# Values as the stationary operand in the attentions of layers 0 and 1

## The chip, the cores and the metric

The kernel runs on one core of a Trainium2 chip. A core has five engines that run side by side: TensorE (PE in the profile, its weight loads PEld), VectorE (DVE), ScalarE (ACT), GpSimd (POOL) and SyncE (SP), which issues most transfers. TensorE multiplies: a stationary operand is loaded (LDWEIGHTS), a moving one streams past it (MATMUL), and the result goes to PSUM, eight banks of 128 partitions by 512 floats. The metric is the device time of one execution in microseconds.

## The reference, cut to what matters

A first block of two layers on 256 tokens and 256 context tokens, then a second block of two layers. Each of the first two layers mixes with attentions of 8 heads of 64. Layer 0 has a recurrence (gated delta rule) beside a latent attention (`blocked_attention`) for all 512 tokens; layer 1 has a neighbourhood attention with a bias and a grouped-query attention (again `blocked_attention`, 2 key/value heads) for the 256 tokens alone. What is computed in each:

```python
s = jnp.einsum('bqkgd,bskd->bkgqs', q_i, k).astype(jnp.float32) * scale
p = jax.nn.softmax(s, axis=-1).astype(v.dtype)
return jnp.einsum('bkgqs,bskd->bqkgd', p, v)
...
s_loc = jnp.einsum('bqhd,bqnhd->bhqn', q_i, kg).astype(jnp.float32) * scale + b_i[None]
s_ctx = jnp.einsum('bqhd,bshd->bhqs', q_i, k_ctx).astype(jnp.float32) * scale
p = jax.nn.softmax(jnp.concatenate([s_loc, s_ctx], -1), axis=-1).astype(v.dtype)
...
y_lat = jnp.concatenate([c_lat.reshape(b, s_len, -1), d_lat.reshape(b, s_len, -1)], -1) @ w_out
```

The concatenated heads go into the output projection `w_out`. The second block's attention is a third one, which the change leaves as it is.

## The kernel before, in words

Tokens are worked on in tiles of 128. Activations that feed a projection are held features by tokens, each as a rounded part ("hi") and a rest ("lo"), and a product in that form is three instructions, high by high, high by rest, rest by high (`mm3`, lines 549 to 551). `split` makes the two parts: a cast on ScalarE, a subtraction on VectorE.

`attend` does one attend: a pair of heads, one tile of 128 tokens. For each head it gets the scores (tokens by keys, 256 or 512 keys) in a PSUM bank, takes the row's maximum on VectorE (L672), the exponential on ScalarE with its sum (L674), transposes the probabilities on TensorE in blocks of 128 (L677) and copies them to SBUF, one head's on ScalarE (L682), the other's on VectorE (L680). Then it multiplies with the values (L688): the transposed probabilities, 128 keys by 128 tokens, are the stationary operand, the values, 128 keys by 64, the moving one, and the result in bank "po" is tokens by 64. VectorE takes the reciprocal of the sums (L691) and multiplies while it takes the result out of PSUM (L692). Probabilities and values are plain 32-bit floats, for which each product is two instructions in the trace. So that the output projection can use it, the result is later transposed (`out_features`, L701) and split.

`l0_mla` (layer 0) goes over four pairs of heads and, in each, over the four token tiles: 16 attends, the tiles of the context with 256 keys, the others with 512. Its scores contract over 128 rows. It is traced after the recurrence (`gdn_run`) and before the last modulation products (`mod_chunk`, L372, bank "gv"). `l1_mixer` has `na(t)` and `gqa(t)` for the two token tiles, four pairs each: 16 attends with 512 keys. Their scores contract over 64 rows, the two heads of a pair in partitions 0 to 63 and 64 to 127. The order in the program: a part of the projections, `na(0)`, the rest of the projections, `na(1)`, the transposes of the grouped keys and queries (`pairs_T`, L1318, bank "aux"), `gqa(0)`, `gqa(1)`.

The order in which each engine gets its instructions is not the program's. A planner simulates the program before the run, prefers what stands earlier in it, but takes what is ready, and hands out buffers as they come free (`tc.tile_pool` with a number of buffers per tag). Each engine then works through its own queue in that fixed order. In layer 1 the banks are "acc" 2, "aux" 1, "s" 2, "tp" 2, "po" 1; in layer 0 "g" 3, "s" 2, "tp" 1, "po" 1, "gv" 1. SBUF tiles "p" and "pt" have two buffers each. The weights of the next stage are loaded when this stage's buffers are closed.

Of the kernel before, what the change touches and what calls it, by code (L numbers as in the profile page):

```python
# [132 lines left out]
def cut(K, shape, dt=F32, tag=None, bufs=1):  # L133
    return sbt(K, shape, dt, tag, bufs, K.cur)
# [74 lines left out]
def aux(K):  # L209
    return bank(K, "aux")  # L210
# [446 lines left out]

def attend(K, pair, t, score, v, O, kinds=("s", "s", "tp", "tp")):  # L660


    nc = K.nc
    sm = cut(K, [128, 2], F32, "sm", 4)
    pts = []
    for hh in range(2):
        h = 2 * pair + hh
        ps, nmx = score(h, t, bank(K, kinds[hh]))
        n = ps.shape[-1]
        if nmx is None:  # L670
            nmx = cut(K, [128, 1], F32, "nmx", 6)
            nc.vector.tensor_reduce(nmx, ps, axis=AX.X, op=ALU.max, negate=True)  # L672
        p = cut(K, [128, 512], F32, "p", K.np)
        nc.scalar.activation(p[:, :n], ps, AF.Exp, bias=nmx, accum_out=sm[:, hh:hh + 1])  # L674
        tp = bank(K, kinds[2 + hh])
        for j in range(n // 128):
            nc.tensor.transpose(tp[:, j * 128:(j + 1) * 128], p[:, j * 128:(j + 1) * 128], K.ident)  # L677
        pt = cut(K, [128, 512], F32, "pt", K.np)
        if hh:
            nc.vector.tensor_copy(pt[:, :n], tp[:, :n])  # L680
        else:
            nc.scalar.copy(pt[:, :n], tp[:, :n])  # L682
        pts.append((pt, n // 128))
    po = bank(K, "po")
# [21 lines left out]
def bc(ap, shape, axis):  # L706
    return ap.unsqueeze(axis).to_broadcast(shape)
# [52 lines left out]
def l0_mla(K, O):  # L760

    nc = K.nc
# [48 lines left out]
    for pair in range(4):  # L811
        heads = {}
        for h in (2 * pair, 2 * pair + 1):
            if h % 4 == 0:
                wq = WQ.load(K.ins["w_q"], 0, 2, (h // 4) * 512, 512)
            late = "g" if pair >= 2 else None
            ps = bank(K, late or "acc")
            hs = slice((h % 4) * 128, (h % 4 + 1) * 128)
            for k in range(2):
                mm3(K, ps, wq[0][:, k, hs], wq[1][:, k, hs], qh[:, k, :], ql[:, k, :], k == 0, k == 1)  # L820
            u = cut(K, [128, 512], F32, "p", K.np)
            nc.vector.tensor_tensor(u, ps, K.c("qtab"), op=ALU.mult)
            q1, q2 = cut(K, [128, 512], FR, "q1", 2), cut(K, [128, 512], FR, "q2", 2)
            split(K, q1, q2, u)
            ps = bank(K, late or "acc")
            hs = slice(h * 64, (h + 1) * 64)
            mm3(K, ps[:64, :], wkh[:, 0, hs], wkl[:, 0, hs], ch, cl, True, True)
            k1, k2 = kh[h % 2], kl[h % 2]
            nc.scalar.copy(k1[:64, :], ps[:64, :])
            nc.vector.tensor_tensor(k2[:64, :], ps[:64, :], k1.bitcast(F32)[:64, :], op=ALU.subtract)  # L830
            heads[h] = (q1, q2, k1, k2)
        for t in range(4):
            n = 256 if t < 2 else 512

            def score(h, t, ps):
                q1, q2, k1, k2 = heads[h]
                tk = slice(t * 128, (t + 1) * 128)
                mm3(K, ps[:, :n], q1[:, tk], q2[:, tk], k1[:, :n], k2[:, :n], True, True)
                return ps[:, :n], None
            attend(K, pair, t, score, lambda h, j: vt[:, j, h * 64:(h + 1) * 64],  # L840
                   O[:, t, pair * 128:(pair + 1) * 128], ("s", "g", "tp", "g") if late else ("s", "s", "tp", "tp"))

# [476 lines left out]
    feat_split(K, hi[:, :n, tk], lo[:, :n, tk], ps[:, :n * 128].rearrange("p (q t) -> p q t", q=n), scale)  # L1319


def score_of(K, qh, ql, kh, kl, n, r, tk, ps):
    mm3(K, ps[:, :n], qh[r, tk], ql[r, tk], kh[r, :n], kl[r, :n], True, True)
    return ps[:, :n]


def l1_mixer(K, W, oh, ol):

    nc = K.nc
# [9 lines left out]
    def tok(t):  # L1339
        return slice(t * 128, (t + 1) * 128)  # L1340
# [29 lines left out]
    O = [cut(K, [128, 1024]) for _ in range(2)]  # L1370
    late = []

    def na(t):
        for pair in range(4):
            def score(h, t, ps):
                b = cut(K, [128, 256], F32, "nab", 4)
                nc.gpsimd.dma_start(b, K.ins["rpbx"][h, t * 128:(t + 1) * 128, :])
                r = slice((h % 2) * 64, (h % 2) * 64 + 64)
                ps = score_of(K, qh[:, pair], ql[:, pair], kh[:, pair], kl[:, pair], 512, r, tok(t), ps)
                nc.vector.tensor_tensor(ps[:, 256:], ps[:, 256:], b, op=ALU.add)  # L1380
                return ps, None
            attend(K, pair, t, score, lambda h, j: vn[:, j, h * 64:h * 64 + 64], O[t][:, pair * 128:(pair + 1) * 128], ("s", "acc", "tp", "acc") if t == 1 and pair >= 1 else ("s", "s", "tp", "tp"))

    def gqa(t):
        for pair in range(4):
            g = pair // 2

            def score(h, t, ps):
                r = slice((h % 2) * 64, (h % 2) * 64 + 64)
                return score_of(K, gqh[:, pair], gql[:, pair], gkh[:, g], gkl[:, g], 512, r, tok(t), ps), None  # L1390
            attend(K, pair, t, score, lambda h, j: vg[:, j, g * 64:g * 64 + 64],
                   O[t][:, 512 + pair * 128:640 + pair * 128], ("s", "acc", "tp", "acc"))

    linear_tok(K, W, xs, w, chunks, [(2, 0), (2, 1), (2, 2), (2, 3), (1, 0), (1, 1), (1, 2), (1, 3), (0, 2), (0, 3)],
               consume)
# [441 lines left out]
def layer0(K):  # L1837
# [18 lines left out]
    with Banks(K, {"acc": 5, "aux": 2, "gv": 1}):  # L1856
        with Pool(K, "tmp"):
# [278 lines left out]
```

## Time and profile before

| | |
|---|---|
| time, median of 3 runs | 2174.61 us (2173.92 to 2179.75) |
| the profiled execution | 2177.07 us, its span 2175.3 us |
| mean granted clock of TensorE | 0.934 |
| busy: TensorE, VectorE, ScalarE, GpSimd | 93%, 60%, 42%, 13% of the span |
| HBM traffic | 133 GB/s over the span |

A busy TensorE is not TensorE at its peak: products are pipelined and overlap in the records, so the step from one start to the next tells more than a duration. L12 is line 12 of the kernel. In the tables by stage a clock of 1.00 is 2.4 GHz and 0.50 is 1.2 GHz.

### The profile page before, as it was taken

The numbers are of one execution on the slowest core, as the hardware profiler recorded it, in microseconds if no ns is written. First come the engines' busy times: TensorE is split into PE (matmuls) and PEld (weight loads), VectorE is DVE, ScalarE is ACT, GpSimd is POOL, SyncE is SP. The second block draws the span as 40 slices with busy tenths as digits, with TensorE's granted clock in tenths as the row PEclk, the third lists the DMA queues.
The fourth block names the chain that finished last, engine by engine and source line by source line (L and its number), as shares of the span: only waits on it lengthen the run. The fifth ranks groups of instructions, "written<-read, shape, count | busy, mean of one in ns | idle before, by whom it ended". The sixth has DMA issues, their size and how long they took to land.

```text
span 2175.3 us, 30931 instructions
## 1 busy us (share of the span) xinstructions
PE 2030.8 (93%) x11512; PEld 1663.8 (76%) x11512; DVE 1315.0 (60%) x2743; ACT 917.4 (42%) x1606; POOL 274.2 (13%) x336
## 2 busy tenths in 40 slices
PE   6989799899999999799997999998899999979998
PEld 4778478778877788587775888897688789868886
DVE  5665556777786644637346555674765558466644
ACT  4533443443222233445235443564554345545532
POOL 2111112211000000213012001110300021040000
PEclk9999799899999999898568999998999999979999
DMA  8244631235685532232024664522556534055562
GB/s 279 91 112 117 195 113 45 78 97 165 194 276 179 165 107 88 70 102 64 20 89 150 187 193 134 158 79 88 164 177 194 172 98 134 20 164 165 186 190 69
DMA packets 186950, 291.86 MB, mean 134 GB/s; under 512 B 28472, under 2 KB 75704, under 8 KB 186800
## 3 DMA queue, kind: packets, MB, share of 16 engines
q1 hardware_dynamic: 172720, 272.54, 40.4%
q0 software_dynamic: 5472, 16.13, 2.2%
q10 hardware_dynamic: 8608, 1.23, 0.4%
q8 instruction: 90, 1.47, 0.3%
q14 instruction: 60, 0.49, 0.1%
HBM read 281.44 MB, written 8.41 MB: 133 GB/s over the span
## 4 chain that ended last, share of the span: by engine, by line
PE 85%; DVE 8%; ACT 3%; DMA 2%; issue 2%; POOL 1%; ACTq 0%; SPq 0%; DVEq 0%; POOLq 0%
PE acc L549 19%; PE acc L551 19%; PE acc L550 19%; PE s L549 3%; PE po L688 3%; PE s L551 2%; PE s L550 2%; PE tp L859 2%; PE po L1504 1%; PE tp L1504 1%; PE gv L372 1%; PE aux L701 1%; PE tp L677 1%; PE g L1168 1%; DVE rsy1p L326 1%
## 5 line engine op out<-in xcount | busy, mean ns | idle before, releaser
L272 DVE TENSOR_TENSOR wlo<-wraw,whi 128x512 fp32r<-128x512 f32 (+4 forms) x748 | 466.3, 667 | 301.1 <-ACT whi L270 283.9
L270 ACT CAST whi<-wraw 128x1024 fp32r<-128x1024 f32 (+4 forms) x420 | 413.8, 990 | 482.4 <-PE acc L551 185.2
L549 PE MATMUL acc<-whi,u 128*128 128x512 f32 (+3 forms) x1320 | 513.3, 391 | 29.4 <-ACT u L306 14.0
L551 PE MATMUL acc<-whi,u 128*128 128x512 f32 (+3 forms) x1320 | 510.0, 388 | 1.9 <-DVE u L307 1.8
L550 PE MATMUL acc<-wlo,u 128*128 128x512 f32 (+3 forms) x1320 | 510.7, 389 | 0.0
L549 PEld LDWEIGHTS acc<-whi,u 128*128 128x128 f32 x1320 | 253.9, 193 | 79.7 <-ACT u L306 16.3
L551 PEld LDWEIGHTS acc<-whi,u 128*128 128x128 f32 x1320 | 253.2, 192 | 53.4 <-DVE u L307 4.8
L550 PEld LDWEIGHTS acc<-wlo,u 128*128 128x128 f32 x1320 | 254.0, 193 | 49.2 <-DVE wlo L272 1.7
L549 PE MATMUL acc<-u,whi 128*128 128x512 f32 (+1 forms) x480 | 172.0, 365 | 3.4 <-ACT u L306 3.3
L551 PE MATMUL acc<-u,wlo 128*128 128x512 f32 (+1 forms) x480 | 172.5, 363 | 0.0
L550 PE MATMUL acc<-u,whi 128*128 128x512 f32 (+1 forms) x480 | 172.0, 361 | 0.0
L272 POOL TENSOR_TENSOR wlo<-wraw,whi 128x512 fp32r<-128x512 f32 (+1 forms) x92 | 116.8, 1300 | 428.7 <-ACT whi L270 428.7
L431 DVE SCALAR_TENSOR_TENSOR msum<-mraw,u,msum 128x512 f32<-128x512 f32 x140 | 100.7, 745 | 11.2 <-DMA mraw<-in_w_mod_dram 10.2
L549 PEld LDWEIGHTS acc<-u,whi 128*128 128x128 f32 x480 | 92.3, 194 | 19.0 <-ACT u L306 4.2
L550 PEld LDWEIGHTS acc<-u,whi 128*128 128x128 f32 x480 | 93.1, 194 | 15.2 <-issue 1.7
L551 PEld LDWEIGHTS acc<-u,wlo 128*128 128x128 f32 x480 | 92.8, 194 | 15.1 <-issue 1.7
L307 DVE TENSOR_TENSOR u<-aux,u 128x512 fp32r<-128x512 f32 (+2 forms) x104 | 64.8, 636 | 40.4 <-ACT u L306 40.2
L306 ACT CAST u<-aux 128x512 fp32r<-128x512 f32 (+2 forms) x104 | 55.4, 546 | 76.1 <-PE aux L701 49.1
L688 PEld LDWEIGHTS po<-u,pt 128*128 128x128 f32 x448 | 75.9, 252 | 8.2 <-issue 2.8
L688 PE MATMUL po<-u,pt 128*128 128x64 f32 x448 | 77.8, 333 | 1.2 <-DVE pt L680 1.2
L549 PE MATMUL acc<-whi,dxh 128*128 128x512 f32 x176 | 69.7, 396 | 1.9 <-ACT dxh L306 1.9
L550 PE MATMUL acc<-wlo,dxh 128*128 128x512 f32 x176 | 69.6, 396 | 0.0
(499 smaller groups left out, 3102.9 us busy)
## 6 DMA issues: line engine op xcount, KB each, us to landing
wraw<-in_w_up_dram SPq DMA_DIRECT2D x64, 512.0 KB, 3.8
wraw<-in_w_down_dram SPq DMA_DIRECT2D x64, 512.0 KB, 4.3
mraw<-in_w_mod_dram SPq DMA_DIRECT2D x56, 512.0 KB, 4.8
wraw<-in_w_ffn_down_dram SPq DMA_DIRECT2D x44, 512.0 KB, 3.8
wraw<-in_w_mod_dram SPq DMA_DIRECT2D x40, 512.0 KB, 5.5
wraw<-in_w_ffn_gate_dram SPq DMA_DIRECT2D x48, 256.0 KB, 3.1
wraw<-in_w_ffn_up_dram SPq DMA_DIRECT2D x48, 256.0 KB, 3.4
wraw<-in_w_ffn_gate_dram SPq DMA_DIRECT2D x20, 512.0 KB, 3.8
```

What stands on the lines that cost most here:

```text
L270: self.K.nc.scalar.copy(hi, raw)
L272: e.tensor_tensor(lo[:, k], raw[:, k], hi.bitcast(F32)[:, k], op=ALU.subtract)
L306: (hi_eng or nc.scalar.copy)(hi, src)
L307: nc.vector.tensor_tensor(lo, src, hi.bitcast(F32), op=ALU.subtract)
L326: nc.vector.scalar_tensor_tensor(y, t, -3.0 * a * a, y, op0=ALU.add, op1=ALU.mult)
L431: nc.vector.scalar_tensor_tensor(accs[s], raw[:, k, :], c, accs[s], op0=ALU.mult, op1=ALU.add)
L549: mm(ps, ah, bh, start=start, stop=False)
L550: mm(ps, ah, bl, start=False, stop=False)
L551: mm(ps, al, bh, start=False, stop=stop)
L688: nc.tensor.matmul(po[:, hh * 64:hh * 64 + 64], pt[:, j * 128:(j + 1) * 128], v(2 * pair + hh, j), start=(j == 0), stop=(j == nj - 1))
L859: nc.tensor.matmul(tp[:, t * 128:(t + 1) * 128], x[:, t // 2, t % 2 * 128 + j:t % 2 * 128 + j + 128], dg[j], start=(j == 0), stop=(j == 4))
L1504: nc.tensor.matmul(ps[t][:, c * 128:c * 128 + 128], yp[:, c, t * 128 + j:t * 128 + j + 128] if j < 31 else ones, dg, start=(j == 0), stop= ...
```

## The change

In layers 0 and 1 the values become the stationary operand and the transposed probabilities the moving one, so the result comes out features by tokens. The two heads of a pair write partitions 0 to 63 and 64 to 127 of one bank, block of keys by block of keys in turn. "po" holds the results of four attends side by side (in layer 0 the four tiles of a pair, in layer 1 the four pairs of a tile). The row sums now lie along the wrong axis: `sums_row` takes their reciprocals repeated 64 times along the free axis and multiplies them with the identity, which gives them features by tokens in a second bank ("gv" in layer 0, "aux" in layer 1). Once for four attends this bank is copied to SBUF and "po" multiplied with it. The transposes of `out_features` go for these attentions. In layer 1 `pair_scores` issues the score products of a pair's two heads in turn, and the bias loads stand behind them. The second block is not touched; its attention stays tokens by features.

```diff
-def attend(K, pair, t, score, v, O, kinds=("s", "s", "tp", "tp")):
+def attend(K, score, v, po, rb, c, kinds=("s", "s", "tp", "tp")):
...
-    for hh in range(2):
-        h = 2 * pair + hh
-        ps, nmx = score(h, t, bank(K, kinds[hh]))
+    for hh, ps in enumerate(score([bank(K, kinds[0]), bank(K, kinds[1])])):
...
-    po = bank(K, "po")
-    for hh in range(2):
-        pt, nj = pts[hh]
-        for j in range(nj):
-            nc.tensor.matmul(po[:, hh * 64:hh * 64 + 64], pt[:, j * 128:(j + 1) * 128], v(2 * pair + hh, j),
+    sums_row(K, sm.unsqueeze(1), rb, c)
+    nj = pts[0][1]
+    for j in range(nj):
+        for hh in range(2):
+            nc.tensor.matmul(po[hh * 64:hh * 64 + 64, c:c + 128], v(hh, j), pts[hh][0][:, j * 128:(j + 1) * 128],
                              start=(j == 0), stop=(j == nj - 1))
-    r = cut(K, [128, 2], F32, "rs", 4)
-    nc.vector.reciprocal(r, sm)
-    nc.vector.tensor_tensor(O.rearrange("p (h d) -> p h d", h=2), po[:, :128].rearrange("p (h d) -> p h d", h=2),
-                            bc(r, [128, 2, 64], 2), op=ALU.mult)
+def sums_row(K, sm, rb, c):
+    n = sm.shape[1]
+    r = cut(K, [128, n, 2, 64], F32, "rs%d" % n, 2)
+    K.nc.vector.reciprocal(r, bc(sm, [128, n, 2, 64], 3))
+    for x in range(n):
+        K.nc.tensor.matmul(rb[:, c + x * 128:c + x * 128 + 128], r[:, x].rearrange("p h d -> p (h d)"), K.ident,
+                           start=True, stop=True)
+def pair_scores(K, q, k, n, tk, pss):
+    steps = ((0, 0), (0, 1), (1, 0))
+    for i, (a, b) in enumerate(steps):
+        for hh in range(2):
+            r = slice(hh * 64, hh * 64 + 64)
+            K.nc.tensor.matmul(pss[hh][:, :n], q[a][r, tk], k[b][r, :n], start=(i == 0), stop=(i == 2))
+    return [ps[:, :n] for ps in pss]
+def attended(K, po, rb, hi, lo, k0, t):
+    n = po.shape[-1] // 128
+    y = cut(K, [128, 512], F32, "pt", K.np)[:, :n * 128]
+    K.nc.scalar.copy(y, rb)
+    K.nc.vector.tensor_tensor(y, po, y, op=ALU.mult)
+    tk = slice(t * 128, (t + 1) * 128)
+    split(K, hi[:, k0:k0 + n, tk], lo[:, k0:k0 + n, tk], y.rearrange("p (k t) -> p k t", k=n))
...
+        po, rb = bank(K, "po"), bank(K, "gv")
         for t in range(4):
...
+        nc.scalar.copy(O[:, pair, :], rb)
+        nc.vector.tensor_tensor(O[:, pair, :], po, O[:, pair, :], op=ALU.mult)
...
     def na(t):
+        po, rb = bank(K, "po"), aux(K)
         for pair in range(4):
...
+            def score(pss):
+                out = pair_scores(K, (qh[:, pair], ql[:, pair]), (kh[:, pair], kl[:, pair]), 512, tok(t), pss)
+                for hh in range(2):
+                    b = cut(K, [128, 256], F32, "nab", 4)
+                    nc.gpsimd.dma_start(b, K.ins["rpbx"][2 * pair + hh, t * 128:(t + 1) * 128, :])
+                    nc.vector.tensor_tensor(out[hh][:, 256:], out[hh][:, 256:], b, op=ALU.add)
+                return out
...
+        attended(K, po, rb, oh, ol, 0, t)
...
         gqa(t)
-        for half in range(2):
-            out_features(K, O[t][:, half * 512:half * 512 + 512], oh, ol, half * 4, t)
...
-            for t in range(4):
-                out_features(K, Om[:, t, :], mh, ml, 4, t)
+            for k in range(4):
+                split(K, mh[:, 4 + k], ml[:, 4 + k], Om[:, k])
```

## Rows read from the trace of the kernel before

**Rows 1.** The chain that ended last, by engine, whole span.
```profile
PE 85%; DVE 8%; ACT 3%; DMA 2%; issue 2%; POOL 1%; ACTq 0%; SPq 0%; DVEq 0%; POOLq 0%
```

**Rows 2.** By stage: us, busy PE, PEld, DVE, ACT, POOL, clock, DMA share, GB/s.
```profile
295.00:437.00 142.00, 131.99 (x1258) 110.66 (x1256) 96.06 (x207) 55.53 (x139) 32.89 (x46) 0.95 0.23 72
437.00:452.00 15.00, 12.17 (x62) 9.61 (x62) 9.80 (x16) 7.78 (x12) 0.00 (x0) 1.00 0.49 163
965.00:1011.00 46.00, 45.64 (x288) 37.24 (x286) 33.86 (x121) 23.41 (x47) 15.45 (x29) 1.00 0.33 104
1011.00:1118.00 107.00, 105.03 (x387) 81.90 (x387) 39.53 (x104) 33.85 (x74) 9.23 (x12) 0.51 0.05 15
```

**Rows 3.** The chain by line in 295:437, in 965:1011 and in 1011:1118.
```profile
by line: PE po L688 12.6%; PE g L1168 10.4%; PE g L1179 9.7%; PE g L1161 7.0%; PE tp L677 5.5%; PE s L549 3.9%; ACT p L674 3.5%; PE gv L372 3.5%; PE s L551 3.4%; PE g L1127 3.3%; PE s L550 3.2%; PE g L1129 2.9%; PE g L677 2.7%; PE g L549 2.
...
by line: PE acc L551 20.0%; PE acc L550 19.5%; PE acc L549 18.2%; PE po L688 9.1%; PE tp L677 6.7%; PE s L549 6.5%; issue 4.2%; PE s L551 4.0%; PE s L550 3.6%; PE aux L1318 2.4%; DVE nmx L672 1.5%; ACT phs L1296 1.4%; ACT lx L1358 1.3%; DVE
...
by line: PE po L688 38.2%; PE tp L677 11.6%; PE acc L677 9.4%; PE s L549 7.1%; PE acc L549 6.7%; PE s L551 4.7%; PE s L550 4.4%; PE acc L550 4.0%; PE acc L551 4.0%; PE aux L701 3.8%; PE aux L1318 2.0%; issue 1.6%; ACT L674 1.2%; DVE pt L680
```

**Rows 4.** Timeline of TensorE, 1076 to 1086 us: start, us, instruction, count.
```profile
1076.35 1.97 PE L688 MATMUL po<-u,pt 128*128 128x64 f32 x8
1078.11 0.42 PE L701 MATMUL aux<-const_id,u 128*128 128x128 f32 x1
1078.32 1.81 PE L688 MATMUL po<-u,pt 128*128 128x64 f32 x8
1079.92 1.06 PE L677 MATMUL acc<-const_id,p 128*128 128x128 f32 x4
1080.91 0.79 PE L549 MATMUL acc<-u,u 64*128 64x512 f32 x1
...
1082.49 1.11 PE L677 MATMUL tp<-const_id,p 128*128 128x128 f32 x4
...
1085.11 1.11 PE L688 MATMUL po<-u,pt 128*128 128x64 f32 x4
```

**Rows 5.** Timeline of TensorE, 316 to 330 us.
```profile
317.06 1.07 PE L372 MATMUL gv<-wraw,u 128*32 128x512 f32 x8
318.05 1.16 PE L1161 MATMUL g<-u,gwq 128*128 128x128 f32 x8
...
325.72 1.04 PE L372 MATMUL gv<-wraw,u 128*32 128x512 f32 x2
```

**Rows 6.** Timeline of TensorE, 995 to 998 and 1005 to 1010 us.
```profile
996.00 0.49 PE L549 MATMUL s<-u,u 64*128 64x512 f32 x1
...
996.89 0.50 PE L551 MATMUL acc<-whi,u 128*128 128x512 f32 x1
...
1006.98 0.50 PE L549 MATMUL s<-u,u 64*128 64x512 f32 x1
1006.99 0.50 PE L549 MATMUL acc<-u,u 64*128 64x512 f32 x1
...
1007.89 0.33 PE L1318 MATMUL aux<-const_id,lkd 128*128 128x128 f32 x1
```

**Rows 7.** Groups by line and shape, 1011:1118: count | busy, mean ns | idle before.
```profile
L549 PE MATMUL s<-u,u 64*128 64x512 f32 x11 | 8.5, 777 | 0.0
L549 PE MATMUL acc<-u,u 64*128 64x512 f32 x10 | 7.9, 792 | 0.0
L680 DVE COPY pt<-acc 128x512 f32<-128x512 f32 x11 | 7.6, 692 | 8.9 <-PE acc L677 8.9
L682 ACT COPY pt<-tp 128x512 f32<-128x512 f32 x12 | 7.0, 586 | 21.8 <-PE po L688 13.6 <-PE tp L677 8.2
L691 DVE RECIPROCAL rs<-sm 128x2 f32<-128x2 f32 x12 | 2.0, 165 | 6.5 <-ACT p L674 6.5
```

**Rows 8.** The instructions of line 930: duration ns min/median/max, first and last start.
```profile
L930 DVE RECIPROCAL u<-u x1: 555/555/555, 64.1 to 64.1; 128x64 f32<-128x64 f32 x1
```

**Rows 9.** Line 1318 likewise, its transposes of grouped keys.
```profile
L1318 PE MATMUL aux<-const_id,lkd x8: 271/374/473, 984.9 to 1027.5; 128*128 128x128 f32 x8
```

More of the change, by code (lines that the diff above doesn't have):

```diff
@@ L665, in attend @@
     pts = []
-    for hh in range(2):
-        h = 2 * pair + hh
-        ps, nmx = score(h, t, bank(K, kinds[hh]))
+    for hh, ps in enumerate(score([bank(K, kinds[0]), bank(K, kinds[1])])):
         n = ps.shape[-1]
-        if nmx is None:
-            nmx = cut(K, [128, 1], F32, "nmx", 6)
-            nc.vector.tensor_reduce(nmx, ps, axis=AX.X, op=ALU.max, negate=True)
+        nmx = cut(K, [128, 1], F32, "nmx", 6)
+        nc.vector.tensor_reduce(nmx, ps, axis=AX.X, op=ALU.max, negate=True)
         p = cut(K, [128, 512], F32, "p", K.np)
@@ L831, in l0_mla @@
             heads[h] = (q1, q2, k1, k2)
+        po, rb = bank(K, "po"), bank(K, "gv")
         for t in range(4):
             n = 256 if t < 2 else 512
-            def score(h, t, ps):
-                q1, q2, k1, k2 = heads[h]
+            def score(pss):
                 tk = slice(t * 128, (t + 1) * 128)
[L838 to L841, printed above, removed]
+                for hh in range(2):
+                    q1, q2, k1, k2 = heads[2 * pair + hh]
+                    mm3(K, pss[hh][:, :n], q1[:, tk], q2[:, tk], k1[:, :n], k2[:, :n], True, True)
+                    yield pss[hh][:, :n]
+            attend(K, score, lambda hh, j: vt[:, j, pair * 128 + hh * 64:pair * 128 + hh * 64 + 64], po, rb, t * 128,
+                   ("s", "g", "tp", "g") if late else ("s", "s", "tp", "tp"))
+        nc.scalar.copy(O[:, pair, :], rb)
+        nc.vector.tensor_tensor(O[:, pair, :], po, O[:, pair, :], op=ALU.mult)
 def gdn_conv(K, W, f0, nf, silu, tensor):
@@ L1319, in pairs_T @@
     feat_split(K, hi[:, :n, tk], lo[:, :n, tk], ps[:, :n * 128].rearrange("p (q t) -> p q t", q=n), scale)
-def score_of(K, qh, ql, kh, kl, n, r, tk, ps):
-    mm3(K, ps[:, :n], qh[r, tk], ql[r, tk], kh[r, :n], kl[r, :n], True, True)
-    return ps[:, :n]
 def l1_mixer(K, W, oh, ol):
@@ L1369, in l1_mixer, with score @@
     chunks = [(0, 512), (512, 512), (1024, 512), (1536, 512), (2048, 256)]
-    O = [cut(K, [128, 1024]) for _ in range(2)]
     late = []
     def na(t):
+        po, rb = bank(K, "po"), aux(K)
         for pair in range(4):
[L1375 to L1382, printed above, removed]
+            def score(pss):
+                out = pair_scores(K, (qh[:, pair], ql[:, pair]), (kh[:, pair], kl[:, pair]), 512, tok(t), pss)
+                for hh in range(2):
+                    b = cut(K, [128, 256], F32, "nab", 4)
+                    nc.gpsimd.dma_start(b, K.ins["rpbx"][2 * pair + hh, t * 128:(t + 1) * 128, :])
+                    nc.vector.tensor_tensor(out[hh][:, 256:], out[hh][:, 256:], b, op=ALU.add)
+                return out
+            attend(K, score, lambda hh, j: vn[:, j, pair * 128 + hh * 64:pair * 128 + hh * 64 + 64], po, rb, pair * 128,
+                   ("s", "acc", "tp", "acc") if t == 1 and pair >= 1 else ("s", "s", "tp", "tp"))
@@ L1384, in gqa, with score @@
+        attended(K, po, rb, oh, ol, 0, t)
     def gqa(t):
+        po, rb = bank(K, "po"), aux(K)
         for pair in range(4):
             g = pair // 2
[L1388 to L1392, printed above, removed]
+            def score(pss):
+                return pair_scores(K, (gqh[:, pair], gql[:, pair]), (gkh[:, g], gkl[:, g]), 512, tok(t), pss)
+            attend(K, score, lambda hh, j: vg[:, j, g * 64:g * 64 + 64], po, rb, pair * 128, ("s", "acc", "tp", "acc"))
@@ L1394, in l1_mixer @@
+        attended(K, po, rb, oh, ol, 4, t)
     linear_tok(K, W, xs, w, chunks, [(2, 0), (2, 1), (2, 2), (2, 3), (1, 0), (1, 1), (1, 2), (1, 3), (0, 2), (0, 3)],
```

## The prediction

> **What bounds the kernel now.** First the chain of waits over the whole span [rows 1]: TensorE carries 85% of it, VectorE 8%. So TensorE time is path, not cover, where the chain runs through it. Where the attentions lie comes from the busy table by stage [rows 2]: in 295 to 437 us (layer 0) they fill the steps of the delta-rule recurrence and then run alone; in 965 to 1011 us (layer 1, first token tile of the neighbourhood attention) they alternate with projections; in 1011 to 1118 us (its second tile, then all the grouped-query attention) they are nearly alone. The reader is to see two things in the last row: TensorE is busy 105.0 of 107 us, VectorE 39.5, ScalarE 33.9, DMA 5%; and the granted clock is 0.51, the lower of the two levels, 1.2 GHz, where the stretch before had 1.00. The chain by line in each stretch [rows 3] gives L688, the product of probabilities and values, 12.6% of 142 us, 9.1% of 46 and 38.2% of 107: 17.9, 4.2 and 40.9 us, 63 together.
>
> TensorE's order in the last stretch [rows 4] shows one attend (two heads, one token tile) from 1076.35 to 1085.11: 8.76 us, and twelve of these are 105 us, the stretch itself. In it: 16 instructions of L688 (8 products, each two instructions in this type) 3.4 us, one transpose of L701 0.21, twice four transposes of L677 about 1.0 each, and twice three score products of 64 rows at 1.58 us a head (1080.91 to 1082.49).
>
> **The change, part by part.** *Products turned round (L688).* The count of products stays; each holds 64 columns of values and streams 128 tokens, where it held 128 and streamed 64. Alone it would cost about as before: eight of L688 take 1.81 us at half the clock [rows 4], eight of L1161, which hold 128 and stream 128, 1.16 at the full one [rows 5]. The gain can only come from two heads writing different halves of the partitions at once. The trace has such products: L372 holds 32 columns of 128 rows and writes four partition groups. Two instructions of one group take 1.04 us; eight over four groups take 1.07, not four times 1.04 [rows 5]. So different groups run together, with different streamed operands. The gain lies between nothing (each head's products by themselves) and half. Half is 20.5 us in the last stretch and 2.1 in the middle one, where TensorE is busy throughout and I take it whole; of 9 us in layer 0 I take 5, because there the recurrence waits for other engines too and the two heads' probabilities come at different times. Sum 27.6.
>
> *Scores of layer 1, two heads in turn.* One head's three products of 64 rows take 0.89 us at the full clock (996.00 to 996.89); once the planner already put two heads side by side, and the six took 0.91 (1006.98 to 1007.89), each pair starting 10 ns apart [rows 6]. So a pair costs what one head does. In the last stretch 21 heads are issued singly [rows 7], 10.5 pairs at 1.57 us, 16.5 us; in the middle stretch 11 of layer 1's 32 heads remain, two pairs of them already so (the other at 971.42), so 3.5 pairs at 0.87, 3.0 us. Layer 0's scores use 128 rows and stay.
>
> *Transposes of the result.* 16 in layer 1 go (L701, 0.21 us each, 1078.11 to 1078.32 [rows 4]): 3.4 us. The 16 in layer 0 cost half that each, 1.8 in all, but sit in 437 to 452 us, where TensorE is busy 12.2 of 15 and DMA 49% [rows 2]: I take 1.0, bounds 0 and 1.8. The casts behind them stay, reading from other buffers.
>
> *The row of sums.* 32 new products of 128 by 128, two instructions each: between L688's step (1.60 us for eight at half clock, so 0.20 a product at the full one, [rows 4]) and L1161's (0.29); I take 0.22, and 0.43 at 1.2 GHz. Twelve at the low clock 5.2, twenty at the full one 4.3: 9.5 us lost, bounds 5 (layer 0's sixteen in gaps) and 13.
>
> *VectorE.* The reciprocal is now taken over 128 elements: 2 cost 165 ns [rows 7] and 64 cost 555 [rows 8], so about 0.96 us (an estimate along that line). In 1011 to 1118 VectorE is 37% busy and the 0.8 more is covered by TensorE's work; at the full clock it would not be. In layer 0 VectorE is busy 96 of 142 us, and some of it stands before a copy that a product awaits: 2 us lost, bounds 0 and 13 (16 times 0.8).
>
> *Ends of a tile.* Layer 1 now evacuates a whole tile at once, a copy of 0.59 and a multiplication of 0.69 [rows 7], and the next tile's first product waits for that bank; the copy also takes one of two "pt" buffers until the split has read it. Three such ends of up to 1.3 us in series, plus a probability copy held up: 1.5 us each, 4.5, and 0.5 for layer 0, whose pair ends have the next pair's projections as cover. Bounds 0 and 9. The 16 bias loads (POOL's queue) are now traced behind the score products; four buffers run ahead, so nothing.
>
> *A bank held longer.* The sums hold "aux" for a whole tile of layer 1. The six transposing steps of keys and queries for the grouped-query attention (L1318), which before slipped in from 984.9 us on [rows 9], must find it free between two tiles, or wait until the second tile ends and then go through one bank, each with its cast and subtraction: about 1.9 us apiece (0.6, and twice 0.6 to 0.7 by [rows 7]). Nothing to 11 us; I take 3. In layer 0 "gv" is held likewise; the modulation products, still running at 325.72 [rows 5], have the gaps between pairs, and their result is due only behind 437: nothing, or one chunk of some 6 us in the open.
>
> Sum: 27.6 + 19.5 + 4.4 - 9.5 - 2 - 5 - 3 = 32 us off. The profiled execution took 2177.07 us (span 2175.3); 32 less is 2145. The median of the runs shown is 2.5 lower: **2143**.
>
> A rule speaks against it. Between L372 and L1161, which divide the array differently, the next begins before the last has ended (317.06 plus 1.07 is behind 318.05, [rows 5]), while the 64-row scores at the low clock take 1.58 us for three times 512 columns, 1.28 us at 1.2 GHz: 0.30 for in and out, and 0.25 at the full clock. The Trainium skill (TensorEngine Tiling (Array Packing), Key Properties) says that switching the tiling mode drains TensorE. By it the half-column products would pay 0.30 in 12 attends and 0.25 in 20, 8.6 us (an estimate), and the sum would be 23; by the rows of L372 it is 32.
>
> **The rivals.** *The clock comes back in 1011 to 1118.* The stretch stays at 0.51 although TensorE is hardly idle, while layer 0's, idle 10 us of 142, has 0.95 [rows 2]; its scores fill all 128 rows. Scores and products that fill both halves of the array together may bring it back. For: that comparison. Against: transposes and sums still stand between. An attend would then cost not 5.7 us (8.76 less 1.7, 1.57 and 0.21, plus 0.43) but about 4, between VectorE's 3.0 (three of 0.69 and 0.96) and 5.7: 12 times 1.7 is 20 more, **2123**.
>
> *Every change of division is paid*, 0.30 us for in and out of the half-column products in 12 attends and 0.25 in 20, as the scores pay: 8.6 us less, **2152**. For: the scores' 0.30. Against: L372.
>
> *The heads are issued apart.* The planner puts instructions where their operands are ready; one head's probabilities come through ScalarE, the other's through VectorE. If half of the products pair up, 32 becomes 18; if only the products do and no scores, 12.5; if only scores, 4.4: **2156 to 2170**.
>
> *No pairing at all.* Then 47 us of the sum are gone, the sums, ends and bank remain: 15 slower, **2190**. It decides where under a third of the pairs run together. Against it: two pairs of scores already do [rows 6].
>
> *Hidden anyway.* The stage behind could absorb the gain if it waited for DMA. In the last stretch DMA is 5% busy [rows 2], so no transfer sets its end; I leave it no chance of its own.
>
> **How the numbers follow.** Chances: the sum as it stands (2130 to 2150) 0.40; the clock back 0.27; changes paid 0.05; heads partly apart 0.15, of which 0.02 within 0.3%; a bank in the open on top of poor pairing, no difference, 0.03; no pairing 0.10. 0.3% is 6.5 us, about what a measurement of this kernel can tell from no change: 2168 to 2181 is the same. Faster 0.85, same 0.05, slower 0.10. The range takes in the clock case with its uncertain attend, and the partly paired ones up to that bound: 2112 to 2168.
>
> **What would show it.** In the profile after: pairs of value products starting together and their share of the chain in the last stretch halved; score products of two heads 10 ns apart throughout layer 1; no transposes of L701's kind there and 64 new sum instructions; the granted clock of that stretch, which parts the first two cases; TensorE gaps at the ends of tiles under 2 us. Wrong would make it: products of one head in runs of eight; a gap of 5 us or more before the grouped-query attention; VectorE's longer reciprocal on the chain.

## The result and the profile after

The changed kernel took 2238.5 us (median of four executions, 2234.1 to 2245.2), the kernel before 2176.4 (2173.9 to 2179.8): a ratio of 1.029 with a 95% interval of 1.025 to 1.032. Slower by some 62 us, where some 32 us less had been forecast. On another chip, beside further runs, the two again took 2238.2 and 2173.0 us. The profiled execution after took 2235.7 us, 58.6 more than that of before.

Its chain of waits by engine is the first reading, against [rows 1]: DMA went from 2% to 5%, which no edit of the change explains.

```profile
PE 79%; DVE 8%; DMA 5%; issue 3%; ACT 3%; POOL 1%; SPq 0%; ACTq 0%; DVEq 0%; POOLq 0%
```

Four events that both kernels have, taken from the first and last starts of single lines, place the loss (in us; the last column is the stage that ends with the event):

| start of | before | after | stage longer by |
|---|---|---|---|
| layer 0's output projection (w_out), first product | 437.6 | 519.1 | 81.5 |
| layer 0's down projection, first product | 761.1 | 851.6 | 9.0 |
| layer 1's last product of probabilities and values | 1116.3 | 1182.2 | -24.6 |
| last product of the kernel | 2169.2 | 2227.8 | -7.3 |

So in these two profiles the stage that holds layer 1 is 24.6 us shorter, near what was expected of it, and 90 us are lost ahead of layer 0's down projection. (The change does not reach the last stage; over all profiles of this case it takes 1044.9 to 1053.5 us.) The stages of layer 0 show where: busy time by stage, after, columns as in [rows 2], and then the same stretch of before.

```profile
200.00:300.00 100.00, 82.59 (x1192) 69.15 (x1191) 52.49 (x144) 43.58 (x94) 16.25 (x33) 0.85 0.33 87
300.00:438.00 138.00, 128.00 (x1146) 103.11 (x1149) 93.72 (x171) 49.20 (x123) 28.93 (x40) 0.88 0.08 24
438.00:520.00 82.00, 48.07 (x149) 12.84 (x141) 10.05 (x22) 8.26 (x14) 4.78 (x9) 0.61 0.53 168
```

```profile
438.00:520.00 82.00, 76.27 (x443) 66.37 (x442) 59.96 (x142) 40.67 (x78) 13.08 (x10) 0.98 0.34 107
```

Up to 438 us the two kernels keep their engines about equally busy, but DMA share and clock are lower after: 0.08 and 0.88 from 300 to 438, where [rows 2] has 0.23 and 0.95. Then come 82 us in which VectorE works 10, ScalarE 8, and TensorE 48, most of it at half the clock. What runs there is read from the groups by line of that stretch (count | busy, mean ns | idle before and its releaser):

```profile
L372 PE MATMUL gv<-wraw,u 128*32 128x512 f32 x96 | 35.3, 983 | 29.4 <-DMA wraw<-in_w_mod_dram 21.6 <-DVE mrow L381 7.3 <-DVE mcols L388 0.5
L374 ACT COPY mrow<-gv 128x512 f32<-128x512 f32 x6 | 3.5, 586 | 66.9 <-PE gv L372 66.9
```

These are the modulation chunks 4 to 9, whose products go through the bank "gv". Line 374 copies each chunk's result, ten in all; its row after and before (duration min/median/max, first and last start) says it shortest:

```profile
L374 ACT COPY mrow<-gv x10: 579/586/587, 21.4 to 516.7; 128x512 f32<-128x512 f32 x10
```

```profile
L374 ACT COPY mrow<-gv x10: 579/586/588, 21.0 to 328.9; 128x512 f32<-128x512 f32 x10
```

Before, the six late chunks were copied out between 219.6 and 328.9 us, inside the recurrence, although the program has them behind the attention. Now all six come behind it. The instructions that touch gv from 430 to 520 us, after, give the order to the microsecond: the last sums of the last pair at 436.5, their copy at 436.8, the first chunk's product at 437.8.

```profile
L372 PE MATMUL gv<-wraw,u x96: 592/1061/1063, 437.8 to 515.6; 128*32 128x512 f32 x96
...
L695 PE MATMUL gv<-const_id,rs x6: 275/275/377, 430.9 to 436.5; 128*128 128x128 f32 x6
...
L867 ACT COPY u<-gv x1: 586/586/586, 436.8 to 436.8; 128x512 f32<-128x512 f32 x1
```

What stands behind the chunks on SP's queue waits as well. The waits of SP's queue from 200 to 520 us (engine and line, releaser: us, times, longest) and the loads of w_out show it: they are issued from 514.1 us, where before the first was out at 328.9.

```profile
SPq L369 <- PE gv L372: 117.6, 19, 77.3
```

```profile
L276 SPq DMA_DIRECT2D wraw<-in_w_out_even_dram x8: 367/368/368, 514.1 to 540.2; - x8
```

In layer 1 the values' products run as forecast: sixteen instructions of two heads (two records are missing in the second row) take 1.9 us at half the clock, where they took 3.4. The scores don't: three of one head and three of the other follow each other. This is TensorE's timeline after, at half the clock and then at the full one; the columns are those of [rows 4].

```profile
1146.88 1.65 PE L705 MATMUL s<-u,u 64*128 64x512 f32 x3
1148.46 1.97 PE L685 MATMUL po<-pt,u 128*64 128x128 f32 x14
1150.36 1.12 PE L674 MATMUL acc<-const_id,p 128*128 128x128 f32 x4
1151.40 1.65 PE L705 MATMUL acc<-u,u 64*128 64x512 f32 x3
...
1153.25 0.64 PE L695 MATMUL aux<-const_id,rs 128*128 128x128 f32 x2
...
1154.46 0.79 PE L705 MATMUL s<-u,u 64*128 64x512 f32 x1
...
1160.91 0.96 PE L705 MATMUL s<-u,u 64*128 64x512 f32 x3
1161.80 0.49 PE L695 MATMUL aux<-const_id,rs 128*128 128x128 f32 x2
1162.22 1.09 PE L685 MATMUL po<-pt,u 128*64 128x128 f32 x16
...
1163.83 0.96 PE L705 MATMUL acc<-u,u 64*128 64x512 f32 x3
...
1165.31 0.96 PE L705 MATMUL s<-u,u 64*128 64x512 f32 x3
```

An attend takes 7.58 us at half the clock (1146.88 to 1154.46) where it took 8.76 [rows 4], and 4.40 at the full one (1160.91 to 1165.31). Only 4 of layer 1's 16 attends have their two heads' scores in turn. Between the second neighbourhood tile and the grouped-query attention there is a hole: the transposing steps of keys and queries (L1345, L1318 of before [rows 9]) go through the bank "aux" one by one, each waiting for its cast and subtraction.

```profile
1126.35 0.44 PE L1345 MATMUL aux<-const_id,lkd 128*128 128x128 f32 x2 [0.53 <-ACT pt L713]
1127.71 0.44 PE L1345 MATMUL aux<-const_id,lkd 128*128 128x128 f32 x2 [0.92 <-DVE u L307]
1129.07 0.54 PE L1345 MATMUL aux<-const_id,lkd 128*128 128x128 f32 x2 [0.92 <-DVE u L307]
1130.54 0.69 PE L1345 MATMUL aux<-const_id,lkd 128*128 128x128 f32 x2 [0.92 <-DVE u L307]
1132.23 1.09 PE L1345 MATMUL aux<-const_id,lx 128*128 128x128 f32 x4 [1.01 <-DVE u L307]
```

By stage (columns as above) VectorE is the busiest engine of the second tile (22.9 of 27 us), then comes the hole (TensorE 8.0 of 13), then the grouped-query attention, first at half the clock, then at the full one.

```profile
1098.00:1125.00 27.00, 22.20 (x132) 14.92 (x133) 22.89 (x58) 11.94 (x26) 12.20 (x15) 0.75 0.14 39
1125.00:1138.00 13.00, 8.00 (x39) 4.56 (x35) 3.89 (x8) 3.79 (x8) 0.00 (x0) 0.66 0.12 41
1138.00:1160.00 22.00, 20.83 (x78) 13.64 (x78) 9.88 (x14) 7.07 (x17) 0.00 (x0) 0.50 0.00 1
1160.00:1183.00 23.00, 21.88 (x171) 14.97 (x169) 14.98 (x21) 11.11 (x26) 0.00 (x0) 1.00 0.00 1
```

Beside the experiments the kernel before took from 2136 to 2193 us, so the medians below are over all executions of a kernel, while a ratio with an interval compares only those within 1.5% of each kernel's fastest.

### The profile page after: what moved, and what is told of

Its sections match the earlier page's. It is cut to its first block, busy times and chain, and to the rows that moved or that the text cites. A ratio compares the mean times of both kernels' runs of the same rounds, so it can differ in the third digit from the quotient of the medians.

```text
span 2233.9 us, 30955 instructions
## 1 busy us (share of the span) xinstructions
PE 2040.7 (91%) x11544; PEld 1639.0 (73%) x11544; DVE 1334.9 (60%) x2719; ACT 920.5 (41%) x1612; POOL 271.8 (12%) x336
## 4 chain that ended last, share of the span: by engine, by line
PE 79%; DVE 8%; DMA 5%; issue 3%; ACT 3%; POOL 1%; SPq 0%; ACTq 0%; DVEq 0%; POOLq 0%
PE acc L549 18%; PE acc L551 18%; PE acc L550 18%; PE s L549 2%; PE s L550 2%; PE s L551 2%; PE gv L372 2%; PE po L1526 1%; DMA wraw<-in_w_mod_dram 1%; PE po L685 1%; PE tp L1526 1%; PE tp L886 1%; PE aux L724 1%; PE g L1195 1%; PE tp L674 1%
## 5 line engine op out<-in xcount | busy, mean ns | idle before, releaser
L307 DVE TENSOR_TENSOR u<-aux,u 128x512 fp32r<-128x512 f32 (+2 forms) x96 | 59.3, 631 | 40.7 <-ACT u L306 40.5
L372 PE MATMUL gv<-wraw,u 128*32 128x512 f32 x160 | 50.9, 933 | 30.0 <-DMA wraw<-in_w_mod_dram 21.6
L306 ACT CAST u<-aux 128x512 fp32r<-128x512 f32 (+2 forms) x96 | 50.7, 543 | 63.6 <-PE aux L724 35.4
L551 PE MATMUL acc<-whi,dxl 128*128 128x512 f32 x176 | 69.5, 399 | 0.0
```

What stands on the lines that cost most here:

```text
L306: (hi_eng or nc.scalar.copy)(hi, src)
L307: nc.vector.tensor_tensor(lo, src, hi.bitcast(F32), op=ALU.subtract)
L372: nc.tensor.matmul(ps[32 * j:32 * j + 32, :], K.cl[:, g + k, :], raw[:, k, :], start=(g + k < 4), stop=(g + k >= 4))
```

## The experiments

### Is it the order of the bank?

*All six chunks ahead of the attention in the program, nothing else:*

```
+ for n in range(4, 10):
+     mod_chunk(K, W, K.po, 0, n)
  l0_mla(K, Om)
- for n in range(4, 10): ...
```

> The kernel after, with the six modulation chunks 4 to 9 of layer 0 put ahead of the attention in the program; nothing else differs. Theory (the bank gv goes round in program order, so in the kernel after the six chunks wait for the sums of the last pair): the chunks run within 200 to 335 us again, w_out's first product comes back from 519 to 440 to 455 us, and the time is 2238 less 80 to 90, 2148 to 2160; up to 20 more if the first pair's sums now wait for the last chunk. Rival (the turned products, the sums and VectorE's longer reciprocals slow layer 0 themselves): over 2200 us.

Measured 2161.8 us (2152.2 to 2174.8); before beside it 2171.8; ratio 1.003 (0.998 to 1.007). *Layer 0's sums in one of the three banks g:*

```
- po, rb = bank(K, "po"), bank(K, "gv")
+ po, rb = bank(K, "po"), bank(K, "g")
```

> The kernel after, with layer 0's sums in one of the three banks g in place of gv. Theory of the bank's order: the chunks run within the recurrence again and the time is 2148 to 2165 us; if the recurrence and the projections, which share g, are held up by it, up to 2180. Rival (layer 0's own new work is what costs): over 2200 us.

Measured 2162.7 us (2159.6 to 2178.8); ratio 1.005 (1.000 to 1.009). *The kernel before, with the bank held and no product turned:*

```
+ rb = bank(K, "gv")                    # per pair of heads
  for t in range(4):
      ...
+     nc.tensor.matmul(rb[:, 2 * t:2 * t + 2], K.ident, sm, start=True, stop=True)
+ nc.vector.tensor_copy(cut(K, [128, 8], F32, "held", 1), rb[:, :8])
```

> The kernel before, to whose layer-0 attention only this is added: each pair of heads takes the bank gv, 16 small products (identity by the two columns of sums) write into it, and one small copy reads it at the pair's end. No product is turned, no scores change. Theory: the six chunks go behind the attention all the same and the time is 2176 plus 75 to 90, 2250 to 2266 us. Rival (the turned products are what costs): 2176 to 2183 us.

Measured 2252.8 us (2242.6 to 2253.2); ratio 1.040 (1.033 to 1.047). Line 374 in the three kernels, in this order:

```profile
L374 ACT COPY mrow<-gv x10: 580/585/587, 20.3 to 325.8; 128x512 f32<-128x512 f32 x10
```

```profile
L374 ACT COPY mrow<-gv x10: 578/586/587, 21.4 to 328.2; 128x512 f32<-128x512 f32 x10
```

```profile
L374 ACT COPY mrow<-gv x10: 581/586/587, 21.4 to 501.4; 128x512 f32<-128x512 f32 x10
```

The theory holds both ways. With the chunks' turn on gv moved or the sums elsewhere, the last chunk is done at 326 to 328 us and 76 us of the loss are gone; with nothing but the hold put into the kernel before, 81 us over its median are there and the last chunk comes at 501.4. A bank with one buffer is handed out in the order of the program, and not simply as it comes free: a chunk that stands behind the last pair can't have it before the last pair has let it go, however early its operands are ready. The 9 us of the table's second row come with the hold as well: with it alone the stretch from w_out to the down projection takes 334.7 us, after 332.5, before 323.5.

### What is left of layer 0's half

*Three chunks ahead of the first pair, one ahead of each later pair:*

```
+ mods(3 if pair == 0 else 1)
  po, rb = bank(K, "po"), bank(K, "gv")
```

> The kernel after, with three of layer 0's six late modulation chunks ahead of the first pair of heads in the program and one ahead of each later pair, so that the bank gv goes to chunks and sums in turn. With all six ahead the recurrence ended some 11 us later than before (403 against 392 us) and w_out began at 453.5 against 437.6 us. Theory (the sums of the first pair waited for the sixth chunk): w_out begins at 438 to 446 us and the time is 8 to 15 below that kernel's, 2145 to 2155 us. Rival (VectorE's sixteen reciprocals and the shared banks po and gv per pair delay layer 0 anyhow): w_out at 450 us or later, 2158 to 2166 us.

Measured 2163.6 us (2161.1 to 2165.5); w_out begins at 445.2 us. That is earlier than the 453.5 with all chunks first, but the whole is no faster: neither theory fits both numbers. In the nine profiles whose layer 0 is that of before, w_out begins anywhere from 435.4 to 446.2 us, so 445.2 cannot be told from before, and the two cures above (453.5 and 452.3) are late by 6 us or more. *The same with the reciprocal over two numbers a partition, in both layers:*

```
- r = cut(K, [128, n, 2, 64], ...); K.nc.vector.reciprocal(r, bc(sm, [128, n, 2, 64], 3))
- K.nc.tensor.matmul(rb[:, c + x * 128:...], r[:, x].rearrange("p h d -> p (h d)"), K.ident, ...)
+ r = cut(K, [128, n, 2], ...); K.nc.vector.reciprocal(r, sm)
+ for hh in range(2):
+     K.nc.tensor.matmul(rb[hh * 64:hh * 64 + 64, c + x * 128:...],
+                        r[:, x, hh:hh + 1].to_broadcast([128, 64]), K.ident, ...)
```

> The kernel with the chunks between the pairs (both layers changed, 2163.6 us), and the reciprocals in both layers over 128 by 2 numbers, spread over 64 columns by the weight load. In layer 1 the short reciprocal was worth nothing (2156.6 against 2151.6, l0's down projection to the last product 328.6 against 329.2). Theory (in layer 0 the sixteen times 0.79 us on VectorE are what delays w_out from some 438 to 441 to 445 us): 4 to 10 less, 2153 to 2160. Rival (the banks po and gv, held for a pair, or the chunks' places): within 3 us of 2163.6.

Measured 2150.7 us, but from 2139.0 to 2174.6. Between 300 and 442 us VectorE's busy time fell from 98.2 to 91.0, and w_out begins 3.1 earlier, at 442.1, which lies within that spread too. Of the 10 us between the two profiled executions 7 lie behind layer 1, where nothing was changed. So nothing of the expected 4 to 10 is shown.

### Layer 1 alone

*Layer 0 as before, layer 1 as after:* the old attend, its loop and out_features are put back in layer 0.

> Layer 1 changed as in the kernel after, layer 0 as in the kernel before. By the two traces layer 1 (first product of layer 0's down projection to the last product of values) went from 355.2 to 330.6 us, and the rest behind it is some 7 shorter: 2176 less 25 to 32, 2144 to 2152 us. The sum of the prediction for layer 1 alone was 26 to 31 less, the same time for another reason (scores paired). Rival (layer 1 profited only from what layer 0's delay brought forward, loads of weights for instance): within 10 us of 2176.

Measured 2151.6 us (2148.2 to 2171.0) against 2171.8 at the median; the ratio is 1.002 (0.997 to 1.007). Its layer-1 stage, from layer 0's down projection to the last product of values, takes 329.2 us, 26.0 less than the 355.2 of before. So the gain at the median does not hang on layer 0's delay. But the kernel before, profiled once more (its control below), takes 330.3 us for this stage. By stage (columns as above), the kernel before twice and then this run:

```profile
761.10:1116.30 355.20, 337.92 (x1478) 269.92 (x1479) 173.46 (x412) 137.91 (x240) 43.49 (x58) 0.83 0.22 69
767.80:1098.10 330.30, 312.99 (x1478) 249.92 (x1479) 173.59 (x412) 137.62 (x240) 43.45 (x58) 0.90 0.23 74
761.60:1090.80 329.20, 301.45 (x1496) 231.01 (x1496) 185.57 (x400) 136.86 (x241) 44.04 (x58) 0.92 0.23 74
```

Against the second row TensorE is busy 11.5 us less and idle 10.5 us more (27.8 against 17.3), and the stage is 1.1 us shorter; most of the 26 us is the clock, 0.92 against 0.83. *The values' products head by head:*

```
- for j in range(nj):
-     for hh in range(2):
+ for hh in range(2):
+     for j in range(nj):
```

> Layer 1 changed, layer 0 as before, but the products of values stand head by head in the program, eight instructions of one half of the partitions and then eight of the other. In pairs the 16 take 1.02 us at the full clock and 1.90 at half. Theory (the gain is that two heads run side by side): 2.1 and 3.8 us instead, 16 times some 1.1 to 1.9 us of which a third is covered: 10 to 20 more than 2149.6, 2160 to 2170 us. Rival (the gain is in the shorter weight load of 64 columns, 137 against 192 ns): within 4 us of 2149.6.

Measured 2160.1 us (2158.3 to 2162.8); the stage takes 339.0 us in place of 329.2, at the same mean clock of 0.92. The timeline shows each head's eight instructions alone in the time that sixteen take in pairs (1.09 us at 1162.22 above):

```profile
1077.58 1.09 PE L685 MATMUL po<-pt,u 128*64 128x128 f32 x8
...
1080.08 1.09 PE L685 MATMUL po<-pt,u 128*64 128x128 f32 x8
```

Pairing halves these products exactly; the rival of the shorter weight load, which this run keeps, is out. The Trainium skill (TensorEngine Tiling (Array Packing), When to Use Tiling) gives this change as its recipe for 64 streamed columns, swapped operands and two column tiles; the trace agrees, with 2 times. *Scores head by head:*

```
- for i, (a, b) in enumerate(steps):
-     for hh in range(2):
+ for hh in range(2):
+     for i, (a, b) in enumerate(steps):
```

> Layer 1 changed, layer 0 as before, but the scores of layer 1 stand head by head in the program, as they did before the change; the products of values stay in pairs. In the trace after, 14 of 16 attends issue their scores as three of one head and then three of the other anyhow (s 1160.91, acc 1163.83). Theory (the planner takes each head when its own bank comes free, so the new order of the scores does nothing): within 4 us of the kernel with layer 1 alone changed, 2151.6. Rival (the prediction: pairs save 0.87 to 1.57 us each): 10 to 20 us more, 2162 to 2172.

Measured 2157.1 us (2149.7 to 2167.4); its profile is that of its base up to 1060 us, and then the clock comes back at 1080 in place of 1064. At a mean granted clock of 0.949 to 0.950 both kernels have executions of 2148 to 2152, so the 5.5 us between the medians are put down to the clock, and the scores' order has no cost that can be seen. (The 14 of 16 of that expectation is 12 of 16, counted over all attends.) *Both heads' scores forced together,* on top of the kernel with the keys first (below); the two banks "s" become one tile of two banks, "ss":

```
+ ss = K.ps["ss"].tile([128, 1024], F32, ..., bufs=1)
+ for hh, ps in enumerate(score([ss[:, :512], ss[:, 512:]])):
- for hh, ps in enumerate(score([bank(K, kinds[0]), bank(K, kinds[1])])):
...
```

> The kernel with the keys' transposing steps first (2142.3 us), and the scores of both heads of layer 1 in one tile of two banks, so that both heads' products can only start together; with it the scores have no second buffer. Theory (a pair costs what one head does, 0.9 us at the full clock): up to 0.9 us less in 16 attends where TensorE is the bound, of which half the tiles are; 5 to 12 less, 2130 to 2137. Rival (without a second buffer the next scores wait for both exponentials, and the chain scores, maximum, exponential, transposes sets an attend at some 4.5 us): within 4 us, or up to 15 more.

Measured 2155.9 us (2151.0 to 2162.5), 13.5 over the kernel that it changes. Its timeline:

```profile
1076.07 0.96 PE L742 MATMUL ss<-u,u 64*128 64x512 f32 x6
...
1078.70 0.66 PE L675 MATMUL tp<-const_id,p 128*128 128x128 f32 x4 [0.22 <-ACT p L672]
1080.11 0.40 PE L686 MATMUL po<-pt,u 128*64 128x128 f32 x2 [0.76 <-ACT pt L680]
1080.71 0.65 PE L675 MATMUL acc<-const_id,p 128*128 128x128 f32 x4 [0.20 <-ACT p L672]
1081.30 0.96 PE L742 MATMUL ss<-u,u 64*128 64x512 f32 x6
```

The six products do take what three took, 0.96 us. But an attend now takes 5.23 us (1076.07 to 1081.30) at the full clock, 0.8 more than 4.40: TensorE waits for exponentials and copies, since the next scores have no free bank. The rival holds. The Trainium skill (TensorEngine Tiling (Array Packing), PSUM Bottleneck) warns that, once tiling has made TensorE faster, the copy out of PSUM may become the limit; this attend agrees in part: TensorE waits 0.76 us for such a copy (1080.11), and 0.42 for two exponentials.

*The keys' transposing steps ahead of the second tile, the queries' through the bank tp:*

```
+ for f in early:        # the four pairs_T of the keys
+     f()
  na(1)
  for f in late: f()     # the two of the queries, ps=bank(K, "tp")
```

> Layer 1 changed, layer 0 as before, and the late transposing steps moved: the four for the keys stand ahead of the second neighbourhood tile, the two for the queries go through the bank tp. In the kernel with layer 1 alone changed they took 1038.5 to 1049.4 us, behind the last product of the second tile, and the first grouped-query attend only had its values' products at 1057. Theory (the sums hold aux through the tile): the gap goes, 8 to 14 us less than that kernel's 2149.6 in its profiled execution, 2136 to 2142. Rival (the gap is VectorE's backlog, which is busy 10 of 10 us there): within 4 us of it.

Measured 2142.3 us (2137.1 to 2147.3); the stage takes 319.3 in place of 329.2 us. By stage, from 1038 to 1057 us without the move and then 8 us later with it (its layer 0 ended 8.2 us later), TensorE's idle time of 6.2 us is nearly gone, and most of the stretch is at the full clock:

```profile
1038.00:1057.00 19.00, 12.84 (x48) 7.20 (x43) 7.91 (x13) 6.61 (x15) 0.00 (x0) 0.64 0.08 28
```

```profile
1046.00:1065.00 19.00, 18.49 (x130) 12.23 (x129) 12.15 (x18) 7.89 (x18) 0.00 (x0) 0.95 0.09 30
```

So the 9.9 us are the sums' hold of aux and what the clock gave beside it: 0.93 over the stage in place of 0.92, up to 4 us of them (an estimate: by these two clocks 45 and 53 us of the two stages ran at half the clock, and half of the difference is 4). *The short reciprocal in layer 1 alone, and then on top of the keys first:*

> Layer 1 changed, layer 0 as before, and the reciprocal of the sums taken over 128 by 2 numbers; each head's column is spread over 64 columns by the weight load itself (a stationary operand of stride zero), in two half-width products. VectorE, busy 10 of 10 us from 1010 to 1020 in the kernel with layer 1 alone changed, loses 16 times 0.79 us. Theory (VectorE bounds the second neighbourhood tile): 4 to 8 us less than 2149.6 us, 2141 to 2146. Rival (covered by TensorE, as the prediction had it): within 3 us of 2149.6.

> Layer 0 as before; layer 1 changed, with the keys' transposing steps first and the short reciprocal. The first of these two gave 2142.3 us; the second was worth nothing while the gap behind the second tile stood. Theory (VectorE now bounds the second tile, 9.9 of 10 us busy): 2 to 6 under 2142.3, 2136 to 2140. Rival (still covered): within 3 us of it.

Measured 2156.6 us (2152.7 to 2165.4; stage 328.6 against 329.2) and 2137.9 us (2129.5 to 2142.5; ratio to before 0.991, 0.986 to 0.995). Covered in the first: VectorE is busy 172.6 us in the stage in place of 185.6, and the stage is 0.6 shorter, so the reciprocals do not bound it. The second is 4 under its base, measured on another chip, and its stage takes 318.1 against 319.3: not settled.

### Everything mended, and two controls

> Everything mended in one kernel: both layers' attentions turned as in the kernel after, layer 0's modulation chunks between the pairs, the short reciprocal in both layers, the keys' transposing steps ahead of the second neighbourhood tile. Theory (layer 0's half of the change gains nothing even then, for its attention fills gaps of the recurrence and the pairs hold po and gv longer): 3 to 10 us over the same kernel with layer 0 as before, 2144 to 2156. Rival (the prediction's 6 us for layer 0, bank aside): 3 to 8 under it, 2132 to 2140.

Measured 2143.2 us (2135.9 to 2160.5; ratio 0.993, 0.988 to 0.999), 5 over the same with layer 0 as before, on one chip. Layer 0's half is worth nothing even mended; the kernel with layer 1 alone changed and mended has the lowest median of all, 35 us under before.

> The kernel after, unchanged, on the chip of these runs. Theory: the 2238.5 us of its first executions again within 10 us, w_out at 515 to 522 us. Rival (its time moves with the clock as that of the kernel before does, 2136 to 2193 us): single executions 20 us or more apart.

Measured 2238.2 us (2231.3 to 2243.3), w_out at 510.4, some 5 us ahead of what was expected. The loss stays.

> The kernel before, unchanged, with a profile of its own. Of the 32 executions of it beside the other runs, 9 took 2136 to 2151 us at a mean granted clock of 0.944 to 0.955, the others 2160 to 2193 at 0.925 to 0.941. Theory (the clock of the last stretch of layer 1 comes back in some executions of one and the same program): times in both groups, and a profile that shows either 0.51 from 1011 to 1118 us or a part of it at 1.00, the span shorter by half of that part's length. Rival (the short ones come from elsewhere in the kernel): a short execution with that stretch at 0.51.

Measured 2173.4 us, from 2144.2 to 2185.4. (Of the 32 executions of that expectation the record has 8, not 9, from 2136 to 2151 us.) The profiled execution of 2159.2 us has the last stretch in two parts, by stage (columns as above), with the same work in the kernel before's first profile under it:

```profile
1010.00:1066.00 56.00, 54.46 (x219) 42.09 (x220) 29.85 (x91) 22.70 (x46) 14.43 (x17) 0.58 0.10 31
1066.00:1098.00 32.00, 31.97 (x218) 25.21 (x217) 16.39 (x33) 13.67 (x33) 0.00 (x0) 0.99 0.00 1
```

```profile
1059.00:1118.00 59.00, 58.23 (x218) 46.13 (x217) 16.69 (x34) 14.34 (x34) 0.00 (x0) 0.50 0.01 1
```

The last 218 records of TensorE take 32 us at 0.99 and 59 at 0.50, TensorE busy throughout in both, in one and the same program. The theory of the clock holds for this execution. It also gives an attend of the kernel before at the full clock, 4.82 us, to be held against 4.40 after:

```profile
1075.33 0.49 PE L549 MATMUL s<-u,u 64*128 64x512 f32 x1
...
1080.15 0.50 PE L549 MATMUL s<-u,u 64*128 64x512 f32 x1
```

## Why the prediction was wrong, point by point

**The step that failed** is the one on the bank "gv": "the modulation products, still running at 325.72 [rows 5], have the gaps between pairs, and their result is due only behind 437: nothing, or one chunk of some 6 us in the open". All six chunks came into the open, 76 to 81 us. The rows that it rested on showed chunks that run ahead of their place in the program; the step took this as freedom to run in any gap, where it was freedom only as long as nothing ahead of them in the program wanted the same single bank. And "due only behind 437" left out that w_out's loads follow the chunks' on SP's queue. The rivals had this bank only as part of another mishap, with 0.03.

**Products turned round** were right in mechanism: two heads take the time of one. Undone, it costs layer 1's stage 9.8 us, where the sum had 22.6. Part of the stretch ran at the full clock, where the products cost half, and in the second tile TensorE waits for other engines; how much each of the two takes is not shown. For layer 0 the sum had 5 us of gain, which no run shows; its terms for layer 0 come to nothing together (5 and 1.0 less 3.4 for the sums, 2 and 0.5).

**Scores in pairs**, 19.5 us of the sum, did not happen in 12 of 16 attends, since the planner takes each head when its own bank is free. That is the rival of heads issued apart, for the scores alone. So an attend fell from 8.76 to 7.58 us at half the clock, where the sum had 5.7, and from 4.82 to 4.40 at the full one, where the rival of the clock had about 4. Where the scores were forced together the pair cost one head's time, as forecast, and the attend grew.

**The row of sums** costs more than the 0.22 and 0.43 us of the sum: 0.42 at the full clock (1161.80 to 1162.22). The prediction's 0.29 for a product among its like is a duration; by starts it is 0.25 (eight instructions, four products, of L1161 from 318.05 to 319.05 in the kernel before). The 0.17 between them point to the rival of paid changes of division, at two thirds of its price; no run separates it. **The reciprocal** takes 0.95 us as estimated; in layer 1 it was covered. **The bank aux** was taken at 3 us in a range to 11 and measured 9.9, the clock's part of up to 4 in it.

**The clock coming back** was a rival at 0.27. In the profile after it came back for the last 23 us of 45, and in one execution of the kernel before it came back with no change at all. Of 92 executions of that kernel beside the experiments, 16 have a mean clock of 0.944 or more; of the 52 executions of the seven kernels with only layer 1 changed, 43 have it. At one mean clock there is no gain to see: at 0.950 and 0.951 the kernel before took 2139 to 2145 us, with layer 1 changed 2148 to 2151, and with it mended, at 0.951, 2139 to 2142. (A stretch at half the clock that gets shorter raises the mean by itself, so this is a comparison and no proof.) So layer 1's gain at the median goes with the clock. What in the change brings it back more often is open. It is not the pairing of the products, for head by head all four executions have 0.948 to 0.951; nor is it the hole, for with the keys first all four have 0.948 to 0.954.

**Layer 1 as a whole** came out 24.6 to 26 us shorter than in the first profile of before, where its terms gave 32 (22.6, 19.5 and 3.4, less 6.0 for the sums, 4.5 and 3). That the two are near each other is luck: against the second profile of before only 1 us is left. The step that failed here is "TensorE time is path, not cover": TensorE's time did shrink by 11.5 us, but 10.5 us of waiting took its place; 6.2 us of waiting lie in the hole at aux.

## What to carry to other kernels

Before a step takes a buffer that has only one copy, list everything that stands behind it in the program and uses the same buffer, and see in the trace when that runs now: what runs ahead of its place loses that freedom, with every load queued behind it. Two products side by side in the program are side by side on TensorE only if both banks come free together; forcing it costs the second buffer. And run the unchanged kernel often enough to see whether it has one time or several, profile it in each, and hold the change against the one at its own clock.

## What was not expected of the hardware

A stationary operand whose 64 columns are one column read with stride zero works, and its load takes 135 ns (median). The granted clock of a stretch in which TensorE is hardly idle can be 0.50 (busy 58.2 of 59 us) or 0.99 (32.0 of 32 us), from one execution of a program to the next. The Trainium skill (TensorE: Matmul & The Clock Gate, What's actually happening) says that activity releases the throttle; the 59 us show a TensorE that is busy by the records and not released.
